# Making the up projection's weight sums by adding transfers in DRAM, and loading the latents' weights block by block

## The chip, the cores and the metric

The kernel runs on one core of a Trainium2 chip. Its engines work side by side, each through its own instructions in order: TensorE (PE, matrix products into PSUM), VectorE (DVE), ScalarE (ACT), GpSimd (POOL) and SyncE (SP, which issues most transfers). Transfers run on 16 DMA engines. Those issued by GpSimd go through the software queue, those issued by SyncE through the hardware queue. The metric is the device time of one execution in microseconds, the median of several.

## The reference

One layer of an encoder over 2048 + 256 tokens of width 1024, in float32, in two parts, each with a norm before and after it and a residual:

```python
h = rms_norm(x, g_mix_pre)
z = h @ w_in                       # latents (416 columns), then nq, nk, nv (512 columns each)
a = mla_attention(c_q, c_kv, k_rope, ...)    # long attention: 8 heads, every token with every token
n = neighborhood_attention(nq, nk, nv, na_rpb)   # 8 heads, windows on a 64-wide grid
mix = jnp.concatenate([a, n], axis=-1) @ w_o
x = x + rms_norm(mix, g_mix_post)
h = rms_norm(x, g_ffn_pre)
x = x + rms_norm(conv_ffn(h, w_ffn_up, ffn_conv_w, ffn_conv_b, w_ffn_down), g_ffn_post)

def conv_ffn(x, w_up, conv_w, conv_b, w_down):
    h = x @ w_up                                  # 1024 -> 2 * 2816
    hc = conv_b + (h at t-1, t, t+1) * conv_w     # width-3 convolution over the tokens
    g, u = jnp.split(hc, 2, axis=-1)
    return (jax.nn.gelu(g, approximate=True) * u) @ w_down
```

## The kernel before

Every product is made in three matmuls (`mm3`): each float32 factor is split into a high half (a cast on ScalarE, L95) and a low half (the difference, on VectorE, L96), and high x high, high x low and low x high are summed in PSUM. A scheduler lays down the order in which each engine works; it may take an instruction earlier than the code writes it, once its sources and its buffer are free.

The stages, in microseconds of the trace. The front, 0 to 240: nine blocks of 256 tokens. `norm_tile` loads 128 tokens, takes their squares (ScalarE), the factor (`rs_m` on VectorE, `rs_r` on GpSimd, L110), scales them (`xn`, L252), transposes them on TensorE into `pt` and splits them into `xh` and `xl`. A block then makes the values of all heads (`pv`) and the queries and keys of four heads (`pq`, stored through `qk_hl`). The weights for it come through four raw buffers (`load_w`, L182): W0 (512 columns, 8 loads), W1 and W2 (256 columns, 16 loads), and the second half of queries and keys for later (w3 here, 16 loads). The split x is kept in DRAM (`xs_d`).

The neighbourhood attention, 260 to 697: eight heads of nine grid units in two halves, 18 steps a head. GpSimd fetches the next head's tensors and the kept blocks of x. Beside the attention, TensorE first makes the other four heads' queries and keys (`queries_rest`), and from the middle (step 72) the latents of the long attention (`latents`). Their 416 columns of weights are loaded at step 72 through the `qk_hl` buffers into the place of the queries' weights, and the latents start six steps later.

Preparation and long attention, 697 to 1655, with almost no transfers. Output projection, 1659 to 1908: 18 tiles of 128 tokens; a tile's attention rows `at` are loaded from `att_d`.

The up projection, 1908 to 2940, works in 66 units (three groups of tokens by 22 columns of blocks j). A unit multiplies a 2 x 2 block matrix of weights with one of x by seven products in place of eight: a product m takes a factor of the weights (a raw block or a sum of blocks) and a factor of x, and VectorE and GpSimd put the results together. `ORDER` and `PLAN` give the order of the products, `pz` are their PSUM banks. The weights' factors are needed three times, once in each pass over j, so the sums are kept in DRAM (`ws_d`). `weight_sums` makes them for j = 0 to 5 on GpSimd beside the output projection (L138 loads, L149 sums, L144 stores); for j = 6 to 21 `w_source` makes them on GpSimd in the first pass (L1132) and stores them; the later passes load them (`load_w`, then split in `w_factor`). The down projection follows to 3505.

## Time and profile before

| | |
|---|---|
| median of 3 runs | 3513.39 us (3508.15 to 3514.28) |
| profiled execution | 3507.15 us, of it the span 3505.4 us |
| mean granted clock of TensorE | 0.989 of full speed |
| TensorE busy | 3368.9 us, 96% of the span |
| VectorE, ScalarE, GpSimd busy | 68%, 52%, 39% |
| transfers | 497.24 MB, mean 142 GB/s |
| of it through GpSimd's software queue | 76.10 MB in 35232 packets |

The page cuts the span into 40 slices; a digit is the busy share in tenths. TensorE is at 9 or 8 in almost all of them, so the other engines' times matter only where TensorE waits for them. The DMA digits show the stages: high in the front and the neighbourhood attention, near nothing in the long attention, high again in the output projection, about half in both projections of the second part.

### The profile page before, as it was taken

The page shows a single profiled execution, that of the slowest core. Times are in us where ns is not written, and L with a number is a line of the kernel's source. Part 1 is how long each engine was busy: PE and PEld are TensorE (multiplying, and loading weights), DVE is VectorE, ACT ScalarE, POOL GpSimd, SP SyncE. Part 2 cuts the span into 40 slices and gives each one's busy share as a digit, 9 for nine tenths or more (in the row PEclk, how much of TensorE's full clock was granted, in tenths as well). Part 3 has the DMA queues.
Part 4 walks back from the last instruction along what each step waited for, and adds up shares of the span by engine and source line. Part 5 has one row for each costly group of instructions (what it writes and reads, how often), then busy time and mean ns, then how long its engine had stood idle before and what let it go on. Part 6 is the DMA issues. An engine that isn't in the chain of part 4 may idle for free.

```text
span 3505.4 us, 51290 instructions
## 1 busy us (share of the span) xinstructions
PE 3368.9 (96%) x17806; PEld 2913.6 (83%) x17806; DVE 2385.9 (68%) x3774; ACT 1837.8 (52%) x3463; POOL 1376.2 (39%) x1216
## 2 busy tenths in 40 slices
PE   8999989989999999999989999899999999999999
PEld 7889979967777777766778999899989999888887
DVE  5325555588988888898345999987789776224332
ACT  4225556567777777777234544555555554223121
POOL 0022323157777778775521477632232222000110
PEclk9999999999999999999999999999999999999999
DMA  8789889341000000011995655465546555434553
GB/s 269 253 258 231 213 191 237 122 149 26 13 15 14 16 14 13 18 47 48 267 256 150 195 170 172 144 192 149 149 113 194 151 150 179 149 117 134 187 186 125
DMA packets 338068, 497.24 MB, mean 142 GB/s; under 512 B 69584, under 2 KB 213072, under 8 KB 330832
## 3 DMA queue, kind: packets, MB, share of 16 engines
q1 hardware_dynamic: 302576, 417.87, 39.7%
q0 software_dynamic: 35232, 76.10, 8.6%
q8 instruction: 140, 2.29, 0.3%
q14 instruction: 120, 0.98, 0.1%
HBM read 337.90 MB, written 155.37 MB: 141 GB/s over the span
## 4 chain that ended last, share of the span: by engine, by line
PE 74%; DVE 10%; ACT 6%; DMA 5%; issue 3%; POOL 2%; SPq 1%; ACTq 0%; POOLq 0%; DVEq 0%
PE pz L1291 21%; PE po L122 6%; PE po L120 6%; PE po L121 6%; PE po L646 3%; PE pS L619 3%; PE pg L600 3%; PE pl L647 3%; PE pS L621 3%; PE pS L620 3%; PE pO L448 2%; DVE wl L96 2%; PE pT L120 2%; PE pT L411 2%; PE pT L122 1%
## 5 line engine op out<-in xcount | busy, mean ns | idle before, releaser
L1291 PE MATMUL pz<-xh,wh 128*128 128x386 f32 (+1 forms) x1848 | 633.3, 343 | 20.8 <-DVE hg L1194 11.5
L1291 PE MATMUL pz<-xl,wh 128*128 128x386 f32 (+1 forms) x1848 | 630.2, 341 | 6.1 <-DVE xl L96 5.7
L1291 PE MATMUL pz<-xh,wl 128*128 128x386 f32 (+1 forms) x1848 | 628.8, 341 | 6.0 <-DVE wl L96 6.0
L634 POOL TENSOR_TENSOR acc<-acc,ph 128x512 f32<-128x512 f32 x434 | 568.3, 1309 | 103.8 <-ACT ph L623 82.3
L96 DVE TENSOR_TENSOR wl<-raw,wh 128x512 fp32r<-128x512 f32 (+1 forms) x470 | 444.0, 953 | 36.2 <-ACT wh L95 36.0
L95 ACT CAST wh<-raw 128x512 fp32r<-128x512 f32 (+1 forms) x470 | 288.9, 627 | 235.4 <-PE pz L1291 221.3
L623 ACT ACTIVATE ph<-pS 128x512 fp32r<-128x512 f32 (+1 forms) x528 | 312.4, 592 | 183.5 <-PE pS L621 98.6
L626 DVE TENSOR_TENSOR pl<-pS,ph 128x512 fp32r<-128x512 f32 (+1 forms) x528 | 354.6, 673 | 71.9 <-ACT pS L624 68.3
L110 POOL TENSOR_TENSOR rs_r<-rs_m,mhalf 128x1 f32<-128x1 f32 (+1 forms) x90 | 74.3, 826 | 800.4 <-DVE rs_m L107 800.1
L1291 PEld LDWEIGHTS pz<-xh,wh 128*128 128x128 f32 x1848 | 350.5, 190 | 31.3 <-DVE hg L1194 16.6
L1291 PEld LDWEIGHTS pz<-xl,wh 128*128 128x128 f32 x1848 | 351.1, 190 | 8.1 <-DVE xl L96 7.3
L1291 PEld LDWEIGHTS pz<-xh,wl 128*128 128x128 f32 x1848 | 350.7, 190 | 7.5 <-DVE wl L96 7.4
L602 DVE TENSOR_REDUCE mx<-pg 128x1 f32<-128x512 f32 (+1 forms) x528 | 343.0, 671 | 12.6 <-PE pg L600 10.1
L1241 POOL TENSOR_TENSOR cg<-cg,cu 128x768 f32<-128x768 f32 (+1 forms) x66 | 165.2, 2503 | 445.3 <-DVE cu L1225 324.6
L122 PE MATMUL po<-dh,xr 128*128 128x512 f32 x792 | 311.7, 394 | 0.4 <-DVE xr L96 0.4
L121 PE MATMUL po<-dl,xr 128*128 128x512 f32 x792 | 311.8, 394 | 0.0
L120 PE MATMUL po<-dh,xr 128*128 128x512 f32 x792 | 311.6, 393 | 0.0
L624 ACT ACTIVATE pS<-pS 128x512 f32<-128x512 f32 (+1 forms) x528 | 311.5, 590 | 0.0
L96 DVE TENSOR_TENSOR xr<-xt,xr 128x1408 fp32r<-128x1408 f32 x37 | 60.6, 1639 | 330.8 <-ACT xr L95 330.8
L95 ACT CAST xr<-xt 128x1408 fp32r<-128x1408 f32 x37 | 50.7, 1369 | 382.1 <-PE po L121 368.3
L619 PE MATMUL pS<-ql,kbh 96*128 96x512 f32 (+1 forms) x528 | 215.2, 408 | 5.0 <-DVE pl L626 2.9
L621 PE MATMUL pS<-qh,kbh 97*128 97x512 f32 (+1 forms) x528 | 211.8, 401 | 0.1
(259 smaller groups left out, 7923.6 us busy)
## 6 DMA issues: line engine op xcount, KB each, us to landing
raw<-ws_d SPq DMA_DIRECT2D x250, 256.0 KB, 2.7
raw<-in_w_ffn_up_dram SPq DMA_DIRECT2D x164, 256.0 KB, 3.2
xt<-g_d SPq DMA_DIRECT2D x37, 704.0 KB, 4.4
graw<-g_d SPq DMA_DIRECT2D x35, 704.0 KB, 5.1
g_d<-cg SPq DMA_DIRECT2D x110, 192.0 KB, 2.3
ws_d<-raw SPq DMA_DIRECT2D x80, 256.0 KB, 2.0
xl<-xs_d POOLq DMA_DIRECT2D x18, 1024.0 KB, 8.8
xh<-xs_d POOLq DMA_DIRECT2D x18, 1024.0 KB, 7.1
```

Of the source, the lines that this page charges most:

```text
L95: self.nc.scalar.copy(out=hi, in_=src)
L96: self.nc.vector.tensor_tensor(out=lo, in0=src, in1=hi.bitcast(F32), op=ALU.subtract)
L120: mm(out=out, lhsT=lh, rhs=rh, start=start, stop=False)
L121: mm(out=out, lhsT=lh, rhs=rl, start=False, stop=False)
L122: mm(out=out, lhsT=ll, rhs=rh, start=False, stop=stop)
L602: nc.vector.tensor_reduce(out=u.mx[:, i, c:c + 1], in_=pg[:, :n], axis=AX.X, op=ALU.max)
L619: mm(out=pS[:, :nq], lhsT=u.kh[0:QKD, kc], rhs=u.ql[:, :nq], start=True, stop=False)
L621: mm(out=pS[:, :nq], lhsT=u.kh[:, kc], rhs=u.qh[:, :nq], start=False, stop=True)
L623: nc.scalar.activation(out=ph[:, :nq], in_=pS[:, :nq], func=AF.Exp, scale=scale)
L626: nc.vector.tensor_tensor(out=pl[:, :nq], in0=pS[:, :nq], in1=ph[:, :nq].bitcast(F32), op=ALU.subtract)
L634: eng.tensor_tensor(out=u.acc[:, :nq], in1=ph[:, :nq].bitcast(F32), op=ALU.add, in0=u.p0[:, :nq].bitcast(F32) if j == 1 else u.acc[:, :nq])
L1291: nc.tensor.matmul(out=pz[:, :w], lhsT=l[:, kk, :], rhs=r[:, kk, :w], start=onto is None and kk == 0 and e == 0, stop=kk == 3 and e == 2, ...
```

## The change

The sums of weights are made without an engine: a transfer in DRAM copies one block of all weights of 11 columns j into `ws_d`, a second one adds the other block to it. The products are chosen so that four plain sums are left, of which two are built on another sum. So there are eight copies and eight additions, each of 11 x 128 x 512 numbers (2.88 MB), all issued by GpSimd. The code issues them at steps 20, 160, 270 and 360 of the long attention, four at a time, eight steps apart. What GpSimd did for the sums in the output projection and the first pass goes, with its loads and stores; all 66 units now load their factors alike.

In a unit the order of products is 1, 5, 3, 7, 2, 6, 4; six take a PSUM bank of their own (five before), and of the additions VectorE makes four instead of five and GpSimd one more.

The second half of queries' and keys' weights lies in eight tiles of 128 columns instead of two of 512. The latents' weights are loaded block by block through two buffers of their own (`load_lat`), each into a tile that the queries have left, from twelve steps before the middle on, and the latents start at the middle.

```diff
-        self.ws_d = scratch("ws_d", (NFF, 5, P, 512))
+        self.ws_d = scratch("ws_d", (NFF, 4, P, 512))
...
-    def weight_sums(self, raw_buf, out_buf, todo):
+    def weight_sums(self):
...
-                for m, ((r0, c0), (r1, c1), sign) in enumerate(self.WSUM.values()):
-                    nc.gpsimd.tensor_tensor(out=out[:, m], in0=raw[r0][:, c0], in1=raw[r1][:, c1],
-                                            op=ALU.add if sign > 0 else ALU.subtract)
-                outs.append((j, c, out))
-
-        def step():
-            load()
-            sums()
-
-        def flush():
-            while raws or outs:
-                sums()
-
-        return step, flush
+        block = lambda rc, js: a["w_ffn_up"].rearrange("(r j) p k c -> r j p (k c)", r=2)[
+            rc[0], js, :, 512 * rc[1]:512 * rc[1] + 512]
+        first, stages = [], [[], [], []]
+        for i, (m, (b0, b1)) in enumerate(self.WSUM.items()):
+            for js in (slice(0, 11), slice(11, NFF)):
+                first.append(lambda i=i, b0=b0, js=js: nc.gpsimd.dma_start(out=self.ws_d[js, i], in_=block(b0, js)))
+                src = self.ws_d[js, list(self.WSUM).index(b1)] if isinstance(b1, int) else block(b1, js)
+                stages[max(0, i - 1)].append(
+                    lambda i=i, src=src, js=js: nc.gpsimd.dma_start(out=self.ws_d[js, i], in_=src, accum_op=ALU.add,
+                                                                  max_dma_last_dim=2048))
+        return [first] + stages
...
-            w2 = w_tiles(w2p, 3, 512)
+            w2 = [[w2p.tile([P, KD, P], F32R, name=f"w{2 * f + i}") for i in range(2)] for f in range(4)]
...
-                        load_w(raw_buf, w2, LAT + 512 * (b - 2) + 256, 256, 256 * (b - 2))
+                        load_w(raw_buf, lambda k: [[w[:, k, :] for w in w2[2 * (b - 2) + i]] for i in range(2)],
+                               LAT + 512 * (b - 2) + 256, 256)
...
+            def load_lat(k):
+                raw = lwp.tile([P, LAT], F32, name="raw")
+                nc.sync.dma_start(out=raw, in_=a["w_in"][k * P:(k + 1) * P, 0:LAT])
+
+                def convert():
+                    wlat[k] = w2p.tile([P, 2, LAT], F32R, name=f"w{k}")
+                    self.split(raw, wlat[k][:, 0, :], wlat[k][:, 1, :])
+
+                return convert
...
+                if 0 <= i - (mid - 10) < KD:
+                    lat_w[i - (mid - 10)]()
+                if 0 <= i - (mid - 12) < KD:
+                    lat_w[i - (mid - 12)] = load_lat(i - (mid - 12))
+                if i == mid - 4:
+                    Rest.blocks = {0: fetch(0)}
                 if i == mid:
-                    wlat = [w[:, :, :LAT] for w in w_tiles(w2p, 3, 512)]
-                    Rest.n, Rest.blocks = 0, {0: fetch(0)}
-                    load_w(lambda: st.tile([P, 2, NB], F32, name="qk_hl").rearrange("p a b -> p (a b)"), wlat, 0, LAT)
-                if i >= mid + LATE and Rest.n < 4 * NT:
+                    Rest.n = 0
+                if i >= mid and Rest.n < 4 * NT:
...
+            for q, part in enumerate(self.weight_sums()):
+                for r, f in enumerate(part):
+                    later.setdefault((20, 160, 270, 360)[q] + 8 * r, []).append(f)
...
-        sums, flush = self.weight_sums(lambda: buf(0, 6, 512), lambda: buf(1, 2, 1280),
-                                       [(j, c) for j in range(self.NSUM) for c in range(2)])
...
-            if t < 7:
-                sums()
-                sums()
-            if t == 7:
-                flush()
...
-    ORDER = (1, 5, 3, 4, 2, 7, 6)
-    WSUM = {1: ((0, 0), (1, 1), 1), 2: ((1, 0), (1, 1), 1), 5: ((0, 0), (0, 1), 1), 6: ((1, 0), (0, 0), -1),
-            7: ((0, 1), (1, 1), -1)}
-    WRAW = {3: (0, 0), 4: (1, 1)}
-    XSUM = {1: ((0, 0), (1, 1), 1), 3: ((0, 1), (1, 1), -1), 4: ((1, 0), (0, 0), -1), 6: ((0, 0), (0, 1), 1),
+
+    WSUM = {4: ((0, 1), (1, 1)), 5: ((0, 0), (0, 1)), 1: ((0, 0), 4), 2: ((1, 0), 1)}
+    WRAW = {3: (0, 0), 6: (1, 0), 7: (1, 1)}
+    XSUM = {1: ((0, 0), (1, 1), 1), 3: ((0, 1), (1, 1), -1), 4: ((0, 0), (1, 0), -1), 6: ((0, 0), (0, 1), 1),
             7: ((1, 0), (1, 1), 1)}
     XRAW = {2: (0, 0), 5: (1, 1)}
 
     PARTS = [(0, 770, 384, 0), (768, 770, 384, 768), (1536, 772, 386, 1536)]
 
-    PLAN = [(k, m) for k in range(3 * NFF) for m in (1, 5, 3, 4, 2, 7, 6)]
-    PLAN[4:9] = [(1, 1), (1, 5), (0, 2), (0, 7), (0, 6)]
-    NRAW = 13
-
-    NSUM = 6
+    PLAN = [(k, m) for k in range(3 * NFF) for m in (1, 5, 3, 7, 2, 6, 4)]
+    PLAN[4:9] = [(1, 1), (1, 5), (0, 2), (0, 6), (0, 4)]
+    NRAW = 10
...
-        if self.NSUM <= k < NFF:
-            for rc in {1: [(0, 0), (1, 1)], 5: [(0, 1)], 3: [(1, 0)]}.get(m, []):
-                t = self.blocks[k, rc] = self.ff_raw.tile([P, 4, P], F32, name="raw")
-                nc.sync.dma_start(out=t, in_=a["w_ffn_up"][j + rc[0] * NFF][:, 4 * rc[1]:4 * rc[1] + 4, :])
-            return
...
-        self.nc.gpsimd.tensor_tensor(out=t, in0=self.blocks[k, b0], in1=self.blocks[k, b1],
-                                     op=ALU.add if sign > 0 else ALU.subtract)
-        self.nc.sync.dma_start(out=self.ws_d[k, list(self.WSUM).index(m)], in_=t.rearrange("p a b -> p (a b)"))
...
-        self.w_source(i + 2)
...
+        def value(u):
+            tt(nc.vector, u.hu[:, 1, :u.w], u.b[6][:, :u.w], u.t[:, :u.w], 1)
+            u.cu = conv(u.hu, NFF + u.j, u.n, "u")
+
         def gate(u):
-            tt(nc.vector, u.hg[:, 0, :u.w], u.b[1][:, :u.w], u.v[:, :u.w], 1)
+            tt(nc.vector, u.hg[:, 0, :u.w], u.v[:, :u.w], u.b[7][:, :u.w], -1)
             u.cg = conv(u.hg, u.j, u.n, "g")
             nc.scalar.activation(out=u.cg[:, :, :u.n], in_=u.cg[:, :, :u.n], func=AF.Gelu_apprx_tanh)
-
-        def value(u):
-            tt(nc.vector, u.hu[:, 1, :u.w], u.b[3][:, :u.w], u.t[:, :u.w], 1)
-            cu = conv(u.hu, NFF + u.j, u.n, "u")
-            nc.gpsimd.tensor_tensor(out=u.cg[:, :, :u.n], in0=u.cg[:, :, :u.n], in1=cu[:, :, :u.n], op=ALU.mult)
+            nc.gpsimd.tensor_tensor(out=u.cg[:, :, :u.n], in0=u.cg[:, :, :u.n], in1=u.cu[:, :, :u.n], op=ALU.mult)
...
-            onto = {7: 1, 6: 3}.get(m)
+            onto = {4: 7}.get(m)
...
-            if m in (5, 4) or (m == 1 and k != 1):
+            if m in (1, 5, 7):
                 keep(u, m)
             if m == 3:
                 u.hg = hp.tile([P, 2, 388], F32, name="hg")
                 tt(nc.vector, u.hg[:, 1, :w], u.b[3][:, :w], u.s[5][:, :w], 1)
-            if m == 4:
                 u.v = hp.tile([P, 388], F32, name="v")
-                tt(nc.gpsimd, u.v[:, :w], u.s[4][:, :w], u.s[5][:, :w], -1)
+                tt(nc.gpsimd, u.v[:, :w], u.s[1][:, :w], u.s[5][:, :w], -1)
             if m == 2:
+                u.t = hp.tile([P, 388], F32, name="t")
+                tt(nc.vector, u.t[:, :w], u.v[:, :w], u.b[2][:, :w], -1)
                 u.hu = hp.tile([P, 2, 388], F32, name="hu")
-                tt(nc.vector, u.hu[:, 0, :w], u.b[2][:, :w], u.s[4][:, :w], 1)
-                u.t = hp.tile([P, 388], F32, name="t")
-                tt(nc.vector, u.t[:, :w], u.s[1][:, :w], u.b[2][:, :w], -1)
-                if k == 0:
-                    keep(hidden[1], 1)
+                tt(nc.gpsimd, u.hu[:, 0, :w], u.s[7][:, :w], u.t[:, :w], -1)
```

How the change moves instructions shows at three places. VectorE at the start of the program, before: `rs_m` and `xn` are the norm of a tile, `w0l` to `w2l` low halves of the front's weights.

```order
L107 TENSOR_SCALAR rs_m<-ss 128x1
L252 SCALAR_TENSOR_TENSOR xn<-x,rs_r,g_mix_pre_b 128x1024
L96 TENSOR_TENSOR w0l<-raw,w0h 128x512 x4
L107 TENSOR_SCALAR rs_m<-ss 128x1
L252 SCALAR_TENSOR_TENSOR xn<-x,rs_r,g_mix_pre_b 128x1024
L96 TENSOR_TENSOR xl<-pt,xh 128x8x128
L107 TENSOR_SCALAR rs_m<-ss 128x1
L96 TENSOR_TENSOR w0l<-raw,w0h 128x512 x2
L252 SCALAR_TENSOR_TENSOR xn<-x,rs_r,g_mix_pre_b 128x1024
L96 TENSOR_TENSOR w0l<-raw,w0h 128x512 x2
L96 TENSOR_TENSOR xl<-pt,xh 128x8x128
L96 TENSOR_TENSOR w1l<-raw,w1h 128x256 x2
```

VectorE at the start, after (the rows left out are 28 more of the narrow low halves, `w_82<-raw,w_81` to `w_88<-raw,w_87`, which are the second half of queries' and keys' weights):

```order
L107 TENSOR_SCALAR rs_m<-ss 128x1
L96 TENSOR_TENSOR w0l<-raw,w0h 128x512 x4
L107 TENSOR_SCALAR rs_m<-ss 128x1
L96 TENSOR_TENSOR w0l<-raw,w0h 128x512 x4
L96 TENSOR_TENSOR w1l<-raw,w1h 128x256 x8
L96 TENSOR_TENSOR w2l<-raw,w2h 128x256 x8
L96 TENSOR_TENSOR w_82<-raw,w_81 128x128
L96 TENSOR_TENSOR w_84<-raw,w_83 128x128
L96 TENSOR_TENSOR w_82<-raw,w_81 128x128
...
L96 TENSOR_TENSOR w_88<-raw,w_87 128x128
L233 SCALAR_TENSOR_TENSOR xn<-x,rs_r,g_mix_pre_b 128x1024 x2
```

The norm of the first tile, second in the row before, now stands behind the low halves of all 40 raw loads, and the norms of tiles 0 and 1 stand together.

VectorE at the border of two blocks of the front, before: `v` are a block's values, `qk_hl` the low halves of its queries and keys, `xl` the low half of a normed tile.

```order
L96 TENSOR_TENSOR v<-pv,v 128x8x64 x2
L96 TENSOR_TENSOR xl<-pt,xh 128x8x128
L107 TENSOR_SCALAR rs_m<-ss 128x1
L252 SCALAR_TENSOR_TENSOR xn<-x,rs_r,g_mix_pre_b 128x1024
L197 SCALAR_TENSOR_TENSOR qk_hl<-pq,qk_hl 128x256 x2
L96 TENSOR_TENSOR xl<-pt,xh 128x8x128
L107 TENSOR_SCALAR rs_m<-ss 128x1
L252 SCALAR_TENSOR_TENSOR xn<-x,rs_r,g_mix_pre_b 128x1024
L96 TENSOR_TENSOR qk_hl<-pq,qk_hl 128x256 x2
```

The same place, after:

```order
L96 TENSOR_TENSOR v<-pv,v 128x8x64 x2
L177 SCALAR_TENSOR_TENSOR qk_hl<-pq,qk_hl 128x256 x2
L96 TENSOR_TENSOR qk_hl<-pq,qk_hl 128x256 x2
L233 SCALAR_TENSOR_TENSOR xn<-x,rs_r,g_mix_pre_b 128x1024 x2
L96 TENSOR_TENSOR xl<-pt,xh 128x8x128
L107 TENSOR_SCALAR rs_m<-ss 128x1
L96 TENSOR_TENSOR xl<-pt,xh 128x8x128
```

Before, the norms of the next block (`xn`) stand between the two pairs of `qk_hl`; after, both stand behind the fourth `qk_hl` of the block, and TensorE's transposes of them with them. That is so at the borders after blocks 0, 1, 2, 3, 5 and 6; after blocks 4 and 7 a norm still stands ahead.

GpSimd in the front and at the start of the neighbourhood attention, after: `rs_r` is a norm's factor, `ws_d<-in_w_ffn_up_dram` at L134 a copy and at L137 an addition, `xh` and `xl<-xs_d` fetch a kept block of x, and `q`, `kk`, `kl`, `v` a head's tensors.

```order
L134 DMA ws_d<-in_w_ffn_up_dram 11x128x512
masks.py:199 ISA
masks.py:199 AFFINE_SELECT ident<-ident 128x128
L110 TENSOR_TENSOR rs_r<-rs_m,mhalf 128x1 x2
L134 DMA ws_d<-in_w_ffn_up_dram 11x128x512
L110 TENSOR_TENSOR rs_r<-rs_m,mhalf 128x1 x2
...
L443 DMA xh<-xs_d 128x2048
L443 DMA xl<-xs_d 128x2048
L137 DMA ws_d<-in_w_ffn_up_dram 11x128x512
L200 DMA q<-naq_d 128x512
L203 DMA kk<-nak_d 64x512 x2
L203 DMA kl<-nak_d 64x512 x2
```

Before, GpSimd has only the factors here, and then the fetches and head loads. After, the eight copies stand between pairs of factors, the first ahead of the identity matrix's last step, and the additions stand one by one among the fetches and head loads (the last of the eight in the preparation of the long attention); none is left in the long attention.

## Rows read from the trace of the kernel before

**Rows 1.** The page's chain that ended last, share of the span by engine
```profile
PE 74%; DVE 10%; ACT 6%; DMA 5%; issue 3%; POOL 2%; SPq 1%; ACTq 0%; POOLq 0%; DVEq 0%
```

**Rows 2.** Windows, front: us, busy time (instructions), granted clock, DMA share, GB/s
```profile
0.00:20.00 20.00, 7.81 (x25) 6.11 (x26) 10.68 (x19) 12.36 (x20) 2.75 (x9) 1.00 0.79 268
43.50:240.00 196.50, 193.53 (x1261) 176.17 (x1259) 67.27 (x114) 54.88 (x105) 18.33 (x31) 0.99 0.77 249
120.00:140.00 20.00, 18.14 (x114) 16.66 (x113) 6.13 (x10) 5.74 (x10) 3.23 (x6) 0.91 0.71 212
```

**Rows 3.** Timeline of the start: start, duration, engine, line, idle and releaser
```profile
7.73 2.56 ACT L95 CAST w0h<-raw 128x512 fp32r<-128x512 f32 x4
8.46 1.28 DVE L252 SCALAR_TENSOR_TENSOR xn<-x,rs_r,g_mix_pre_b 128x1024 f32<-128x1024 f32 x1 [0.68 <-POOL rs_r L110]
9.67 2.49 DVE L96 TENSOR_TENSOR w0l<-raw,w0h 128x512 fp32r<-128x512 f32 x4
11.96 0.99 ACT L95 CAST xh<-pt 128x1024 fp32r<-128x1024 f32 x1
13.00 0.80 PE L120 MATMUL pv<-w0h,xh 128*128 128x512 f32 x1 [1.23 <-ACT xh L95]
14.11 1.22 DVE L96 TENSOR_TENSOR xl<-pt,xh 128x1024 fp32r<-128x1024 f32 x1
20.69 0.75 DVE L96 TENSOR_TENSOR w1l<-raw,w1h 128x256 fp32r<-128x256 f32 x2
43.09 0.42 DVE L96 TENSOR_TENSOR qk_hl<-pq,qk_hl 128x256 fp32r<-128x256 f32 x1 [1.08 <-ACT qk_hl L95]
```

**Rows 4.** The raw loads' line: duration min/median/max in ns, first and last start
```profile
L182 SPq DMA_DIRECT2D raw<-in_w_in_dram x40: 327/430/1707, 1.7 to 98.5; - x40
```

**Rows 5.** Windows of the neighbourhood attention's middle, columns as in rows 2
```profile
480.00:520.00 40.00, 26.86 (x150) 24.74 (x151) 20.04 (x46) 21.09 (x51) 7.87 (x13) 0.79 0.92 181
520.00:540.00 20.00, 20.00 (x143) 19.27 (x142) 11.76 (x30) 12.12 (x30) 5.24 (x5) 1.00 0.38 127
```

**Rows 6.** Chain of 470 to 520 us: start, duration, what
```profile
478.16 10.13 DMA qk_hl<-in_w_in_dram
```

**Rows 7.** Windows of the output projection, columns as in rows 2
```profile
1660.00:1820.00 160.00, 142.96 (x676) 117.24 (x677) 68.56 (x95) 45.13 (x71) 70.36 (x93) 0.96 0.93 267
1820.00:1880.00 60.00, 60.00 (x306) 50.63 (x305) 29.11 (x42) 21.46 (x36) 8.32 (x15) 1.00 0.67 180
```

**Rows 8.** TensorE's waits, 1660 to 1820 us: total, times, longest
```profile
PE pt L948 <- DMA at<-att_d: 15.5, 4, 7.1
```

**Rows 9.** Windows of the up projection, columns as in rows 2
```profile
2000.00:2200.00 200.00, 189.32 (x1041) 183.00 (x1040) 200.00 (x199) 94.66 (x162) 150.84 (x87) 1.00 0.53 170
2400.00:2500.00 100.00, 100.00 (x567) 100.00 (x566) 74.22 (x108) 54.92 (x88) 22.78 (x14) 1.00 0.55 152
```

**Rows 10.** Lines, 2000 to 2100 us, then 2400 to 2500: busy, mean ns
```profile
L96 DVE TENSOR_TENSOR wl<-raw,wh 128x512 fp32r<-128x512 f32 x44 | 56.3, 1291 | 0.0
L1132 POOL TENSOR_TENSOR raw<-raw 128x512 f32<-128x512 f32 x31 | 51.8, 1671 | 28.4 <-DVE wl L96 27.5
...
L96 DVE TENSOR_TENSOR wl<-raw,wh 128x512 fp32r<-128x512 f32 x48 | 35.2, 734 | 7.5 <-ACT wh L95 7.5
```

**Rows 11.** The page's DMA issues: times, KB each, median us to landing
```profile
xl<-xs_d POOLq DMA_DIRECT2D x18, 1024.0 KB, 8.8
...
raw<-in_w_in_dram SPq DMA_DIRECT2D x32, 128.0 KB, 3.1
...
raw<-in_w_in_dram SPq DMA_DIRECT2D x8, 256.0 KB, 5.0
```

**Rows 12.** Windows of the neighbourhood attention, columns as in rows 2
```profile
260.00:280.00 20.00, 17.86 (x120) 17.13 (x121) 11.02 (x27) 10.67 (x26) 5.33 (x9) 0.83 1.34 296
280.00:480.00 200.00, 194.40 (x1554) 187.11 (x1553) 113.89 (x277) 112.38 (x273) 57.96 (x83) 1.00 0.83 217
```

**Rows 13.** The fetches of x: duration in ns, first and last start
```profile
L460 POOL DMA_DIRECT2D xl<-xs_d x18: 528/538/576, 216.4 to 660.9; - x18
```

More of the change, by code (lines that the diff above doesn't have):

```diff
@@ L284, in queries @@
                         pq = ps.tile([P, 512], F32, name="pq")[:, :NB]
-                        qk_products(W[1 + f // 2], f % 2, pq, range(KD), xh, xl)
+                        qk_products([w[:, :, f % 2 * P:f % 2 * P + P] for w in W[1 + f // 2]], pq, range(KD), xh, xl)
                         qk_store(f // 2, 2 * (f % 2), pq, b)
@@ L475, in queries_rest @@
                     Rest.pq = ps_t.tile([P, 512], F32, name="pT")[:, :NB]
-                qk_products(w2, f, Rest.pq, range(4 * half, 4 * half + 4), *Rest.blocks[b])
+                qk_products(w2[f], Rest.pq, range(4 * half, 4 * half + 4), *Rest.blocks[b])
                 if half == 1:
@@ L1070, in ffn_pools @@
             self.xc_open(self.up, m)
-        self.xsrc, self.xc, self.raws, self.blocks, self.wf = {}, {}, {}, {}, {}
+        self.xsrc, self.xc, self.raws, self.wf = {}, {}, {}, {}
     def xc_open(self, stack, m, **k):
@@ L1187, in ffn @@
         wp = [en(name="ff_w0", bufs=3), en(name="ff_w1", bufs=5)]
-        for m in (3, 4):
+        for m in (3, 7):
             self.xc_open(right, m, side="right")
@@ L1275, in ffn @@
                 pz_open(2)
-                for q in (2, 7, 6):
+                for q in (2, 6, 4):
                     self.xc_open(self.up, q)
@@ L1313, in ffn @@
                     store = None
-            if m == 7:
-                if k < last:
-                    gate(u)
-                else:
-                    post.append(lambda: gate(u))
             if m == 6:
@@ L1321, in ffn @@
                     value(u)
+                else:
+                    post.append(lambda: value(u))
+            if m == 4:
+                if k < last:
+                    gate(u)
                     store = lambda u=hidden.pop(k): store_of(u)
                 else:
-                    post += [lambda: value(u), lambda: store_of(u)]
+                    post += [lambda: gate(u), lambda: store_of(u)]
         self.up.close()
```

63 lines of the change are left out of this document (17 added, 46 removed).

## The prediction

> **What bounds the kernel now.** I read the chain of waits first: three quarters of it are TensorE's own work [rows 1], so anything that doesn't hold TensorE up is free, and what counts is where TensorE stops. I then looked at the span in windows, one stretch per stage, for the columns that fall below full busy or below full clock. Four places matter here.
>
> The start: TensorE is busy for 7.81 of the first 20 us and then full [rows 2]. The timeline shows why it is so early: the norm of the first tile runs on VectorE at 8.46 us and the low halves of the weights only follow, so that the first product starts at 13.00 and the last store of block 0 is made at 43.09 [rows 3]. The 40 raw loads of projection weights are issued between 1.7 and 98.5 us [rows 4].
>
> The middle of the neighbourhood attention: between 480 and 520 us TensorE does 150 matmuls in 40 us where the next stretch does 143 in 20 [rows 5]; the chain there is a DMA of 10.13 us that brings the latents' weights [rows 6].
>
> The output projection: 676 matmuls in 160 us against 306 in the 60 us after, with the DMA engines at 0.93 of their time [rows 7]; TensorE waits 15.5 us for a load of attention rows [rows 8].
>
> The up projection's first pass: VectorE is busy 200 of 200 us and TensorE does 1041 matmuls; later 567 per 100 us, with VectorE at 74 [rows 9]. A low half of a weight takes 1291 ns there beside GpSimd's sums, and 734 ns without them [rows 10].
>
> **What the change does, part by part.**
>
> *Gains.* (1) The 60 sums in the output projection and their loads and stores go. At the rate of the later stretch (306/60 = 5.1 per us) 676 matmuls take 132.5 us, so 27.5 us are lost [rows 7]. The ends are the 15.5 us of the wait alone [rows 8] and 27.5; I take 25, since the DMA load that the wait stands for goes almost wholly.
> (2) The 80 sums and 80 stores of the first pass go, and the VectorE additions per unit fall from five to four. A unit is 84 matmuls: 84/5.205 = 16.14 us in the first pass, 84/5.67 = 14.81 after it [rows 9]; sixteen units (j = 6 to 21) save 16 x 1.33 = 21 us. Ends 15 and 25 (the two passes' borders could move a few us). The new order of products and the sixth bank add nothing, as TensorE is already full in the later passes.
> (3) The latents' weights come block by block and early. 150 matmuls at 143 per 20 us are 21 us, so 19 of the 40 us are lost [rows 5]; I take 12, as the conversions still stand among the attention's own work, with 3 and 19 as ends.
> Together 58 us, between 33 and 71.
>
> *Cost at the start.* The order of the changed program has the adding transfers not in the long attention, where the code writes them, but as early as their sources allow: the eight copies in the front, the eight additions one by one in the neighbourhood attention. And with the copies among GpSimd's norm factors the whole front comes in another order. On VectorE all 56 splits of projection weights (8 wide, 16 half as wide and 32 narrow ones) now stand ahead of the first norm; SyncE issues all 40 raw loads in one go through four buffers. An engine takes its work in order, so the first norm waits for the last raw load. One buffer's turn is its load, the cast, the split and the issue: for the eight wide loads 5.0 + 0.64 + 0.62 + 0.43 = 6.69 us, of which four run at once, so 1.67 each; for the 32 small ones 3.1 + 0.37 + 0.37 + 0.43 = 4.27, so 1.07 each [rows 3, 4, 11] (of a small cast no row is shown; it is taken to be as long as its split). The first norm starts at 1.7 + 8 x 1.67 + 32 x 1.07 = 49 us, and with two copies beside the loads say 52, against 8.46. From there block 0 runs as before. Cost: 43 us; less 2 for the two tiles of block 1 that block 0 no longer transposes: 41. Lowest: the issues alone (1.7 + 40 x 0.43 = 19) and some 9 us of splits behind them, so 28, which costs 20. Highest: loads that take twice as long beside the copies, near 80, which costs 70.
>
> *Cost at the block borders.* Before, the next block's norms stand between the queries of this one. Now, at six of eight borders (all but 4 to 5 and 7 to 8), they stand behind its last store. TensorE then waits for the cast and the low half (0.42 each, the cast taken to be as long), the norm (1.28), the cast of the transposed tile (0.99) and most of its low half (0.75 of 1.22, as two matmuls go ahead of it): 3.9 us; the transposes between are work that was there before [rows 3]. A stop also costs clock: between 120 and 140 us TensorE stood for 20 - 18.14 = 1.9 us, and the granted clock of that stretch is 0.91, a part of it at 1.2 instead of 2.4 GHz: another 1.8 us [rows 2]. So 6 x 5.7 = 34 us; ends 23 (no clock lost) and 48 (the wait for GpSimd's factor beside it).
>
> *Cost of the transfers.* No row of before shows a copy within DRAM or an adding transfer. Each moves 2.88 MB. From below: at the 296 GB/s of 260 to 280 us, with the DMA engines over full [rows 12], 10 us; that stretch is the nearest row. In the front the engines are busy 0.77 of the time [rows 2], so the copies fit beside TensorE's work, at the price of later loads: I take 4 us (0 to 20). In the neighbourhood attention, 0.83 busy [rows 12], an addition stands in GpSimd's queue ahead of the next block of x or the next head. A block's fetch takes 8.8 us [rows 11], and the fetches come 26 us apart (444.5 us for 17 steps) [rows 13], so a delay of 10 us is mostly covered: 2 us for each of the seven there, with the last in the preparation of the long attention 15. Without that cover, 9 us each, 65; below zero nothing speaks for it, as these transfers release nothing earlier.
> The Trainium skill speaks against them: *Collectives: The Full Stack*, "The bandwidth ceiling: the fold count and why AG ≠ RS ≠ AR", says that an addition in a DMA costs no time itself but reads two sources, so it runs at about half of a copy's rate. No run here shows it; with it an addition would be an estimated 20 us, twice the 10 from the row, and the exposed sum would be nearer to the upper end.
>
> *Sum.* 41 + 34 + 4 + 15 = 94 lost, 58 gained: 36 us slower. The profiled execution took 3507.15 us and would take 3543; the median shown is 6.2 above it, so the forecast is 3549. The long attention, with hardly any DMA, and the down projection stay as they are.
>
> **Rivals.** *The queue is held (B).* Software transfers run one behind another. If an addition takes 20 us or more, or GpSimd can't go on while one is being queued, each of the seven holds a fetch past its block, or a norm's factor in the front. For it: the DMA engines are 0.83 taken there before anything is added [rows 12]. Against it: 26 us between two fetches [rows 13]. It adds 50 us, seven waits of 9 less the 13 already counted: 3600.
> *The front hides it (C), faster or even.* The mechanism is the turn of the four raw buffers: nothing else but two copies uses the DMA engines then, and if the loads land near the issue rate the norm starts at 28 us and the start costs 20. With 23 at the borders and nothing for the transfers, 43 stand against 58: 3513 - 15 = 3498; with the upper gains 3485. The sign turns once start, borders and transfers together cost less than 58 us: with 23 and 4 for the last two that is a first norm before 42 us. For it: four raws are there and being cast at 7.73 us, with the first x [rows 3]. Against it: the splits behind the loads, and the order itself.
>
> **How the numbers follow.** Forecast 0.50, with a range of its own of 3515 to 3590; B 0.25; C 0.25. A run of this kernel varies by about 0.2% (3508 to 3514), so within 7 us counts as the same. Slower takes all of B, 0.45 of the forecast's half and a little of C: 0.72; same 0.06; faster 0.22. The range runs from 3480 (C with good gains) to 3625 (B with 75 us).
>
> **What would show it.** Right at the start: VectorE's first norm near 50 us and TensorE idle until then. At the borders: TensorE waits for xn, six times, 3 to 6 us. In the neighbourhood attention: waits for blocks of x at most a few us each. In the output projection the wait for attention rows gone and the rate over 100 matmuls per 20 us; in the first pass a unit of 14.8 us and VectorE well under full. The prediction is wrong if the first norm is early, if the fetches wait 20 us (B), or if the up projection's first pass keeps its 16.1 us.

## The result and the profile after

The changed kernel takes 3670.89 us (3664.74 to 3671.72) against 3513.02 us: 1.0448 times the time before [1.043, 1.0466]. The sign was forecast, the size not: 158 us lost instead of 36, outside the range.

Where the time went is read by stage, from the first and last start of each stage's products or scores in the two profiles (spans 3505.4 and 3669.5 us):

| stage | before | after | difference | forecast |
|---|---|---|---|---|
| start to the first score of the neighbourhood attention | 250.6 | 365.6 | +115.0 | +79 |
| neighbourhood attention, first to last score | 437.7 | 481.8 | +44.1 | +3 with the next |
| from there to the first score of the long attention | 101.1 | 122.2 | +21.1 | |
| long attention's scores | 862.9 | 862.8 | -0.1 | 0 |
| from the last score to the up projection (output projection) | 258.1 | 257.4 | -0.7 | -25 |
| up projection | 1034.7 | 1017.6 | -17.1 | -21 |
| the rest | 560.3 | 562.1 | +1.8 | 0 |

The front first. Windows of after, columns as in [rows 2]:

```profile
0.00:20.00 20.00, 0.00 (x0) 0.00 (x0) 4.03 (x11) 7.19 (x11) 4.27 (x10) 1.00 0.84 298
20.00:56.00 36.00, 0.00 (x0) 0.00 (x0) 16.88 (x52) 15.49 (x50) 0.00 (x0) 1.00 0.67 214
88.00:366.00 278.00, 230.28 (x1338) 203.37 (x1339) 69.42 (x112) 52.48 (x94) 31.70 (x48) 0.86 0.78 247
340.00:360.00 20.00, 3.83 (x18) 3.83 (x19) 3.95 (x12) 0.75 (x2) 3.83 (x7) 0.63 0.78 194
```

TensorE stands for 56 us, where it was at work from 13 us on [rows 3]. Over the blocks behind the first the mean granted clock is 0.86, where [rows 2] had 0.99, and at the end TensorE all but stops for 20 us. VectorE's timeline names the first stop and the border after block 0:

```profile
55.57 2.48 DVE L233 SCALAR_TENSOR_TENSOR xn<-x,rs_r,g_mix_pre_b 128x1024 f32<-128x1024 f32 x2
...
87.95 0.43 DVE L96 TENSOR_TENSOR qk_hl<-pq,qk_hl 128x256 fp32r<-128x256 f32 x1 [0.23 <-ACT qk_hl L95]
88.29 2.47 DVE L233 SCALAR_TENSOR_TENSOR xn<-x,rs_r,g_mix_pre_b 128x1024 f32<-128x1024 f32 x2
```

The norm starts at 55.57 us (forecast: 52) and block 0 ends at 87.95 against 43.09 [rows 3]. The raw loads answer [rows 4]: all forty now go out by 52.6 us.

```profile
L161 SPq DMA_DIRECT2D raw<-in_w_in_dram x40: 327/328/626, 1.7 to 52.6; - x40
```

The neighbourhood attention, in windows: the whole of it and a stretch of it, then two stretches of the preparation of the long attention, the first all but 4 us ahead of the last addition (876.05 us), the second beside it.

```profile
365.00:847.00 482.00, 437.80 (x3077) 415.15 (x3076) 245.54 (x587) 251.96 (x604) 126.28 (x173) 0.94 1.00 225
600.00:640.00 40.00, 28.42 (x178) 25.55 (x177) 18.07 (x43) 16.89 (x43) 11.56 (x16) 0.90 1.04 228
860.00:880.00 20.00, 7.70 (x31) 6.39 (x32) 7.93 (x27) 9.59 (x35) 13.56 (x29) 0.56 0.33 95
880.00:900.00 20.00, 13.89 (x63) 10.31 (x62) 8.94 (x30) 8.59 (x28) 6.55 (x18) 0.86 0.87 187
```

The DMA share is 1.00 over the whole stage, where [rows 12] had 0.83 at full clock; in 600 to 640 us, after an addition, TensorE does 4.5 matmuls per us against 7.8 there. The transfers' own rows show what GpSimd spends on an issue (ns, min/median/max), the first and last start, and below the time from issue to landing, by line; L134 is the copies, L137 the additions:

```profile
L134 POOL DMA_DIRECT2D ws_d<-in_w_ffn_up_dram x8: 1116/1142/1324, 1.4 to 288.6; - x8
...
DMA to landing us min/median/max: 17.5/20.4/28.1
```

```profile
L137 POOL DMA_DIRECT2D ws_d<-in_w_ffn_up_dram x4: 1995/1998/2003, 312.3 to 594.8; - x4
L137 POOL DMA_DIRECT2D ws_d<-ws_d x4: 1942/1997/2015, 675.7 to 876.1; - x4
...
DMA to landing us min/median/max: 29.2/30.7/43.1
```

A copy needs a median of 20.4 us to land and an addition 30.7, where the forecast had 10. The waits of TensorE up to 1000 us (total, times, longest):

```profile
PE pt L237 <- DVE xn L233: 75.5, 8, 56.9
PE pt L841 <- DVE zn L824: 20.6, 4, 19.3
```

The first row is the start and seven later norms (18.6 us together). The second is the preparation, but 19.3 of its 20.6 us end at 872.30 us, before the last addition is issued; the seventh was issued at 800.41 and landed 30.1 us later. With copies alone (e3 below) TensorE stops for 8.5 us at this place: there VectorE makes the first `zn` behind one low half of the stage's weights, here behind all four, so that it waits for four loads in turn.

```profile
871.18 0.75 DVE L809 SCALAR_TENSOR_TENSOR wkl<-raw,gk,wkh 128x512 fp32r<-128x512 f32 x1 [3.42 <-ACT wkh L808]
871.85 0.35 DVE L824 TENSOR_SCALAR zn<-z,rs_r 128x256 f32<-128x256 f32 x1
```

Some 11 of the 25 us that the preparation loses against e3 thus go with the changed order. Behind the addition issued at 876.05 the chain of after then has two slow loads (start, duration, what); all loads of that table of rotations need 2.2 us at the median.

```profile
886.25 6.27 DMA z<-z_d
...
895.13 11.35 DMA cs<-in_rope_dram
```

In the neighbourhood attention TensorE's waits are spread (the largest group is 17.0 us in six). The chain of after has two additions themselves there, from issue to landing, and behind them GpSimd's loads of a head's keys and values:

```profile
594.79 32.59 DMA ws_d<-in_w_ffn_up_dram
...
675.73 29.41 DMA ws_d<-ws_d
```

The same is seen at GpSimd, which stood ahead of a head's values until an addition had landed, and at ScalarE, which waited for a buffer whose store was late:

```profile
POOL v L205 <- DMA ws_d<-ws_d: 21.2, 1, 21.2
```

```profile
ACT qk_hl L95 <- DMA naq_d<-qk_hl: 17.6, 5, 5.3
ACT o L434 <- DMA natt_d<-o: 14.4, 5, 5.3
```

The output projection and the up projection, windows that answer [rows 7] and [rows 9]:

```profile
1840.00:1860.00 20.00, 7.81 (x26) 5.75 (x27) 3.29 (x11) 1.21 (x2) 1.58 (x4) 0.59 0.67 184
1860.00:2080.00 220.00, 216.47 (x1073) 181.33 (x1072) 100.59 (x148) 72.98 (x120) 34.29 (x51) 0.99 0.61 170
2180.00:2380.00 200.00, 200.00 (x1131) 200.00 (x1130) 155.90 (x202) 110.27 (x173) 61.24 (x41) 1.00 0.50 153
```

The output projection runs at 97.5 matmuls per 20 us once it is going (84.5 before, in its first 160 us); from the first tile's last transposes (`pu`) to the last tile's it took 240.4 us and takes 222. But it now starts with a stop (1840 to 1860) that gives it all back. The first pass of the up projection runs at 5.66 matmuls per us, as forecast, with VectorE at 78%.

### The profile page after: what moved, and what is told of

Its sections match the earlier page's. It is cut to its first block, busy times and chain, and to the rows that moved or that the text cites. A ratio compares the mean times of both kernels' runs of the same rounds, so it can differ in the third digit from the quotient of the medians.

```text
span 3669.5 us, 51097 instructions
## 1 busy us (share of the span) xinstructions
PE 3409.6 (93%) x17806; PEld 2946.7 (80%) x17806; DVE 2332.7 (64%) x3724; ACT 1857.3 (51%) x3479; POOL 1297.4 (35%) x1158
## 4 chain that ended last, share of the span: by engine, by line
PE 73%; DMA 10%; DVE 8%; ACT 4%; issue 3%; POOL 1%; SPq 0%; ACTq 0%; POOLq 0%; DVEq 0%
PE pz L1254 24%; PE po L120 7%; PE po L122 7%; PE po L121 7%; PE po L644 3%; PE pS L617 3%; PE pg L598 3%; PE pl L645 2%; PE pS L619 2%; DMA naq_d<-qk_hl 2%; PE pS L618 2%; PE pO L431 1%; DVE wl L96 1%; DMA raw<-in_w_in_dram 1%; DVE mx L600 1%
## 5 line engine op out<-in xcount | busy, mean ns | idle before, releaser
L1157 POOL TENSOR_TENSOR v<-s,s 128x386 f32<-128x386 f32 (+1 forms) x66 | 101.5, 1538 | 435.7 <-DVE cg L1188 308.0
```

## The experiments

What a kernel leaves out is told in its expectation. Ratios are to the kernel before, on the same chip.

**No transfers: e1_no_transfers.** Theory: the loss sits in the transfers and the order that they bring. Rival: the rest of the change costs too.

```diff
-            for q, part in enumerate(self.weight_sums()):
+            for q, part in enumerate([]):
...
-            nc.sync.dma_start(out=flat, in_=self.ws_d[j, list(self.WSUM).index(m)])
+            r, c = {4: (0, 1), 5: (0, 1), 1: (0, 0), 2: (1, 0)}[m]
+            nc.sync.dma_start(out=t, in_=a["w_ffn_up"][j + r * NFF][:, 4 * c:4 * c + 4, :])
```

> The changed kernel without any of the sixteen transfers; the up projection loads raw blocks in place of the sums (so the weight sums are left out). Theory 1 (the large copies and additions that GpSimd issues, by the order they force and by their traffic, cost the whole loss): the front and the neighbourhood attention go back to the times of before, and the gains are left: about 3455 us (3440 to 3480). Rival (the new weight tiles, the latents' loads and the new order of products cost it): slower than 3513, with the first scores of the neighbourhood attention after 300 us.

Measured: 3473.38 us, 0.9907 [0.9889, 0.9926]. First norm at 8.71 us, first score at 249.3, neighbourhood attention 423.0, preparation 97.3, up projection 1014.6: nearly 200 us lie between this kernel and the changed one, and all of it comes with the sixteen transfers and the order that they bring. The theory's 3440 to 3480 holds. But the output projection's stage still takes 256.6 us, so its missing gain isn't the transfers' doing.

**The latents alone: b1_latents_only**, the kernel before with the weights' tiles and `load_lat` of the change and nothing else.

> The kernel before with the part on the latents' weights alone: tiles of 128 columns, loads block by block, latents from the middle on. From the stages of the kernel without transfers: neighbourhood attention 423 instead of 438 us, preparation 97 instead of 101, the rest as before: about 18 us less than the kernel before, ratio 0.995. Rival (that gain came from the absence of the sums' traffic or from another order): within 5 us of the kernel before.

Measured: 3490.96 us, 0.9956 [0.9944, 0.9969]. The neighbourhood attention takes 423.3 us instead of 437.7 and the preparation 98.2 instead of 101.1. The front of the profiled execution is 6.7 us longer (first score at 257.3), so its span is only 11.3 us shorter; by the medians it is 18. The stretch of [rows 5] is filled:

```profile
480.00:520.00 40.00, 39.77 (x275) 38.36 (x276) 24.67 (x61) 24.95 (x60) 10.30 (x18) 1.00 0.99 234
```

**Copies without additions: e3_copies_only.**

```diff
-            for q, part in enumerate(self.weight_sums()):
+            for q, part in enumerate(self.weight_sums()[:1]):
```

> The changed kernel with the eight copies where they are, without the eight additions (so one block is missing from each sum). Theory 1 and its rival agree on the front: first scores at about 365 us. If the additions cost what the neighbourhood attention and the preparation lost (44 and 21 us) it takes about 3605 us; if those came from the disturbed front order or the latents it stays near 3670.

Measured: 3579.31 us, 1.0202 [1.0186, 1.0219]. First norm at 55.52 us, first score at 351.4, neighbourhood attention 427.5, preparation 97.3. So the eight additions, with the order that they bring, cost 92 us by the spans (3669.5 - 3577.6): 14 at the end of the front (365.6 - 351.4), 54 in the neighbourhood attention, 25 in the preparation. The expectation had missed the first of these. The eight copies and the order of the front cost 106 more than e1 has. Two of ScalarE's waits in the neighbourhood attention, for comparison with after:

```profile
ACT qk_hl L95 <- DMA naq_d<-qk_hl: 9.9, 2, 7.0
...
ACT o L434 <- DMA natt_d<-o: 1.8, 2, 1.1
```

**The front's order without a transfer: e11_order_only**, as e1, with the front written in the changed order and each norm held behind the last low half of the raw loads or of the block before.

```diff
+                    with tc.issue_after(self.gate):
                         nc.vector.scalar_tensor_tensor(out=xn, in0=x, scalar=r[:, 0:1], in1=g,
```

> The kernel without any transfer (sums left out), its front forced into the changed kernel's order: all 40 raw loads and their splits ahead of the first norm, and each block's norms behind the last store of the block before, at all eight borders. Order theory: first norm at 45 to 50 us, first scores of the neighbourhood attention at 249 + 40 + 8 x 5.7 = 335 us, about 3558 us in all. Traffic theory (the copies' bytes made the first norm and the borders late): first scores before 300 us, under 3525 us.

Measured: 3551.39 us, 1.0139 [1.0116, 1.0161]. First norm at 40.26 us, blocks of 29 to 32 us (24.3 to 26.6 before), first score at 329.0: the order alone costs 80 us. It has all eight borders bad, the changed kernel six; without the two further ones (6.7 and 3.9 us) that would be 69. The first norm shows the copies: without them the forty loads are through 15 us earlier.

**Copies without the order: e5b_small_copies_only.** The same bytes, cut into 88 copies of one column j each; so cut, the front keeps its early norm.

```diff
-            for js in (slice(0, 11), slice(11, NFF)):
+            for js in [slice(j, j + 1) for j in range(NFF)]:
```

> As the kernel with copies only, the same bytes, but each copy cut into eleven of one column j, which leaves the first norm ahead of the weights' splits on VectorE and the next block's norms between the queries. Order theory (the place of the norms costs the front, not the copies' traffic): first norm near 8.5 us, first scores of the neighbourhood attention near 260 us, about 3470 us in all. Traffic theory (the copies' bytes slow the front's loads and stores): first scores later than 320 us, over 3540 us.

Measured: 3522.74 us, 1.0045 [1.003, 1.0059]. First norm at 9.92 us, first score at 296.3: between the two theories, the copies alone, so cut, cost 47 us of the front. They don't do it by GpSimd's factors, for which VectorE waits 2.9 us in the first 140 us, but by the front's own transfers: the raw loads of these 140 us need 7.3 us to land at the median, in e1 3.4, ScalarE waits 52 us for them instead of 8, and they are 37% of the chain there. Its window from 43 us on:

```profile
43.00:296.00 253.00, 220.11 (x1396) 200.38 (x1395) 75.83 (x152) 62.53 (x137) 54.59 (x101) 0.93 0.85 292
```

**All transfers cut small: e5_small_hoisted** (the same cut, with the additions). Cut so, the additions move into the front too.

> The changed kernel with all copies and additions as early as the scheduler likes, but each cut into eleven of one column j: the bytes of the changed kernel, an order close to the one without transfers. Against the copies-only version of the same cut (3523 us) only the additions are new. Order theory (what an addition costs in the neighbourhood attention is the order around it): neighbourhood attention 425 us from its first score to its last, preparation 98, about 3525 us in all. Traffic theory (its bytes and its place in the software queue): the 482 and 122 us of the changed kernel, about 3600 us.

Measured: 3604.94 us, 1.0287 [1.0265, 1.0309]; first score at 380.4, then 422.9 for the neighbourhood attention. The order theory had the neighbourhood attention, the traffic theory the total: the additions cost 84 us where they stand, which is now the front (380.4 - 296.3), where e5b's DMA engines are busy 0.85 of the time, and nothing behind it.

**Additions in the neighbourhood attention, TensorE's order kept: e15_additions_in_attention.** The transfers with the 128 rows outermost, each addition held behind a head's tables.

```diff
+        turn = lambda t: t.rearrange("j p c -> p j c")
...
+                    if t in self.sum_at:
+                        with tc.issue_after(self.tables[self.sum_at[t]]):
+                            t()
```

> The changed kernel with all sixteen transfers unchanged in size and number but described with the 128 rows outermost, and the additions held one by one behind a head's tables in the neighbourhood attention, so that they stand at almost the places of the changed kernel while TensorE's order there is almost that of the kernel without transfers (16 lines of difference in the products of that stage; the changed kernel has 392). What is open is whether the 54 us that the additions add in the neighbourhood attention (481.8 against 427.5 with copies only) and the 25 us in the preparation are the transfers' own (they hold GpSimd's queue and the DMA engines, so fetches come late) or come from the other order of TensorE's work. If the transfers' own: natt 470 to 490 us, preparation 115 to 125, GpSimd's fetches behind each addition waiting 15 to 25 us. If the order's: natt 425 to 440, preparation 97 to 105. The front has the copies and part of the bad order: its first score 290 to 330. In total about 3590 to 3620 by the first theory and 3530 to 3560 by the second.

Measured: 3564.06 us, 1.0158 [1.0131, 1.0186]; neighbourhood attention 452.3 us, preparation 97.5. Neither theory had it: 25 us (452.3 against 427.5) are lost beside an order as good as that without transfers; the other 29 go with the changed order or with the shape, which this run changes together (what the shape does to a transfer stands in the last section). On the chain of this run stand three fetches of x behind additions, of 24 to 26 us each, where e3's fetches need 10.5 at most, and TensorE waits 10.7 us for such fetches. The preparation loses nothing once the last addition is issued at 703 us, ahead of it. The window of the stage:

```profile
312.00:764.00 452.00, 423.00 (x3073) 405.73 (x3073) 244.85 (x586) 252.76 (x604) 130.35 (x176) 0.97 1.05 249
```

**In the long attention, as the code writes it: e2_pinned.** Each transfer is held behind GpSimd's last sum of the long attention's weights.

```diff
+                    if t in sums:
+                        with tc.issue_after(self.pool_ins):
+                            t()
```

> The changed kernel with every transfer queued behind a GpSimd instruction of the long attention, at the steps where the code writes it. Theory 1: as without the transfers, about 3460 us (3440 to 3480), since the DMA engines are at 0.08 there; TensorE in the long attention stays at 862 us. Rival (an addition in DRAM is dear wherever it stands, by holding GpSimd or the memory): the long attention takes over 20 us longer than its 862.

Measured: 3558.51 us, 1.0149 [1.0134, 1.0164]. Front and neighbourhood attention are as in e1 (253.9, 422.6), but the long attention takes 946.9 us instead of 862.7. The theory's 3440 to 3480 is missed, and the rival's sign is there. TensorE's order changes around the transfers: up to 13 score products of `pg` in a row, where e1 has at most three.

**Cut small, in the long attention: e7_pinned_small**, e2 with the cut of e5b; TensorE's order is that of e1.

> All transfers in the long attention, as in the pinned kernel, but cut into single columns, so that TensorE's order there is the one without transfers. Order theory: the long attention takes 863 us again instead of 947, about 3475 us in all, as without transfers; if 176 issues on GpSimd are too many for its free fifth, up to 20 us more. Traffic theory (the copies and additions slow the loads of the long attention): it stays near 940 us, over 3545 us.

Measured: 3526.16 us, 1.0066 [1.0044, 1.0088]; long attention 913.3 us. Neither theory had it. The large cut and its order are 34 of the 84 us; the other 51 are lost beside e1's order, and GpSimd is full in the stretches with the 176 issues. That these issues and not the bytes cost the 51 is argued from that, and from e12 below, where the same bytes cost 20. Windows of e7, and of e1 in the same place:

```profile
830.00:930.00 100.00, 93.80 (x405) 66.53 (x406) 83.71 (x146) 72.22 (x141) 98.69 (x113) 0.98 0.50 162
1080.00:1130.00 50.00, 40.44 (x167) 27.44 (x166) 32.90 (x57) 29.00 (x56) 50.00 (x50) 0.89 0.92 141
```

```profile
830.00:930.00 100.00, 98.58 (x444) 70.82 (x442) 88.76 (x156) 75.56 (x147) 80.30 (x63) 1.00 0.06 15
```

**The stores of zeros later: e9_pinned_small_zc**, e7 with the three stores `x_d<-zc` behind the fourth tile of the output projection. They take SyncE 6.55 us at 1844.72 us of after, ahead of the first load of neighbourhood rows:

```profile
1844.72 6.55 SPq L931 DMA_DIRECT2D x_d<-zc x3
1851.31 0.67 SPq L938 DMA_DIRECT2D na<-natt_d  x1
```

> The pinned kernel with small transfers, and the three narrow stores of zeros in the output projection moved behind its fourth tile, out of the way of the first loads of the neighbourhood attention's rows. Theory (the output projection's gain was lost to a late first load behind these stores on SyncE): its time from the last score of the long attention to the first product of the up projection falls from 256 us by 5 to 12 us, about 3466 us in all. Rival (these loads are late by themselves): no change against the pinned kernel with small transfers.

Measured: 3521.9 us, 1.0049 [1.0033, 1.0065]; from the last score to the up projection 250.3 us instead of 255.1. Just under the theory's 5 to 12: a part of the missing 25, not the most.

**Eleven raw buffers: e13_none_eleven_raws**, e1 with one number changed.

```diff
-    NRAW = 10
+    NRAW = 11
```

> The kernel without transfers (sums left out), with eleven raw buffers in place of ten, which in the order brings the output projection's zero stores and first loads back to the start of the long attention. Theory (the number of raw buffers moved these loads behind the last score, and that ate the output projection's gain): from the last score of the long attention to the first product of the up projection 238 us instead of 256, about 3455 us in all. Rival: no change, 3473 us.

Measured: 3462.65 us, 0.9874 [0.9855, 0.9893]; the stage takes 237.4 us instead of 256.6. The stores of zeros are at 784 us again, as before the change (795), and the output projection starts without a stop.

**Put together: e12_pfirst_pinned**, which leaves nothing out: sixteen transfers with the 128 rows outermost, held in the long attention and spread over it (a copy every 20 steps, an addition every 25), and eleven raw buffers.

```diff
+                    later.setdefault(at, []).append(f)
+                    at += (20, 25, 25, 25)[q]
```

> All sixteen transfers in the long attention, as large as in the changed kernel but with the 128 rows as the outermost dimension in place of the eleven columns, spread evenly, and eleven raw buffers in place of ten. With this shape TensorE's order in the long attention is the one without transfers. Theory (a transfer cost order there, and in the small cut GpSimd's issue time, not bytes): the long attention takes 863 to 873 us, and with the raw buffers the output projection gets its early first loads back; 3455 to 3470 us in all, faster than the kernel before. Rival (bytes or queue cost it wherever they go): the long attention over 900 us, 3500 us or more.

Measured: 3480.76 us, 0.9926 [0.9913, 0.9938]: 28 us faster than before on the same chip (3509.06), and some 190 faster than the changed kernel. The long attention takes 884.4 us, 20 more than in e13 and 11 above the theory's upper end, as is the total; the rest is as there. TensorE's order there is not quite the one without transfers: counted over the products in the two traces, it differs from e13's in some 190 lines (e2's from e1's in some 800). How much of the 20 us is order, issue or traffic isn't separated. Its window beside e1's above, and the transfers in this quiet stage:

```profile
830.00:930.00 100.00, 95.73 (x427) 67.66 (x427) 85.69 (x150) 77.01 (x150) 77.86 (x62) 1.00 0.33 102
```

```profile
L135 POOL DMA_DIRECT2D ws_d<-in_w_ffn_up_dram x8: 1064/1067/1143, 794.3 to 1034.6; - x8
...
DMA to landing us min/median/max: 11.7/12.3/13.3
```

```profile
L138 POOL DMA_DIRECT2D ws_d<-in_w_ffn_up_dram x4: 1851/1876/1947, 1064.9 to 1192.7; - x4
L138 POOL DMA_DIRECT2D ws_d<-ws_d x4: 1855/1874/1893, 1233.0 to 1359.2; - x4
...
DMA to landing us min/median/max: 18.8/19.6/20.9
```

## Why the prediction was right and wrong

*Latents, 12 forecast: 17.* The 14.4 and 2.9 us of b1. Right, nearer the upper end.

*Up projection's first pass, 21 forecast: 17.* Right; the rate is that of the later passes. VectorE's low halves still take 887 ns beside GpSimd's work and not 734, which costs nothing, as VectorE no longer sets the pace.

The front's 115 us are, by the ends of the blocks, 45 at the start, 53 at the six borders (7.6 us on average at five, 15.5 at the one after block 3) and 18 at the last block, of which 14 come with the first addition (e3); at the other places it gains 1.

*Start, 41 forecast: 45.* Right in mechanism: VectorE's first norm waits for forty raw loads. That the size is right too is luck in part: the copies beside the loads were put at 3 us and are 15 by e11, and the loads alone were put at 49 us, where the first norm of e11 starts at 40.

*Borders, 34 forecast: 53.* Right in mechanism, too small in size: e11 has 6.6 us a border without a transfer, 39 for these six, against 5.7 and 34. The other 14, for which this term had nothing, come with the transfers, most of them at the border after block 3, where two copies are issued (197 and 214 us) and ScalarE waits 11.4 us for stores of `qk_hl`.

*Copies, 4 forecast.* Mis-sized; their cost lies within the stretches above. Beside the bad order they add 22 (351.4 - 329.0), or 33 if e11's two further borders are taken off, the 15 at the start and the 14 at the borders among them; beside the good order they cost 47. The step that failed is "the copies fit beside TensorE's work": 0.77 of the DMA time taken [rows 2] was read as 0.23 free. But 23 MB are moved in some 300 us in which the front's own loads and stores have to land in time; in e5b the raw loads take 7.3 us instead of 3.4.

*Additions, 15 forecast: 93* (14 + 54 + 25). The largest miss, and the step that failed is "a delay of 10 us is mostly covered". An addition takes 31 us to land, not 10, which is more than the 26 us between two fetches [rows 13], and that cover was worked out for the fetches of x alone. In the changed kernel those hardly stop TensorE (4.0 us); what is late is the rest of GpSimd's queue and of the DMA engines' work: a head's keys and values behind two additions on the chain (32.6 and 29.4 us), stores that hold the `qk_hl` buffers (17.6 us against 9.9 in e3), stores of `o` (14.4 against 1.8), the rotation tables in the preparation. A second step had no term at all: the additions also change the order of the stages in which they stand, and that is some 11 of the preparation's 25 us. The upper end of 65 was built on fetches too, and so too low. Rival B had the mechanism, an addition of over 20 us that holds GpSimd's queue, but priced it by the fetches as well. Of the 54 us in the neighbourhood attention e15 gives 25 to transfers as such; whether the other 29 are the order's (392 lines of difference in TensorE's products) or the shape's isn't separated.

What the prediction drew from the Trainium skill pointed the right way. The Trainium skill, *Collectives: The Full Stack*, "The bandwidth ceiling: the fold count and why AG ≠ RS ≠ AR", says of a ring's ReduceScatter that its addition reads two sources and so runs at about half of a copy's rate; in the quiet long attention of e2 the copies ran at about 290 GB/s and the additions at 143. The 296 GB/s taken from [rows 12] was thus right for a copy, and the estimate of 20 us nearer to the truth for an addition than the 10 taken.

*Output projection, 25 forecast: 1.* The wait for attention rows went and the stage runs 18 us shorter from tile to tile (222 against 240.4), but the start lost as much. The step that failed is that the change's other numbers were put at nothing without a reason: NRAW from 13 to 10 moves the stores of zeros and the first load of rows from 800 us to behind the long attention's last score. Eleven buffers give 19 us of this stage back (e13); the whole kernel gains 11 by the medians (3462.65 against 3473.38), as other stages of the profiled execution are a few us longer. That the number of buffers decides it is shown; by which memory the tiles then share wasn't tried.

Rival C was off from both sides: the first norm came at 55 us, not 28, and the transfers weren't free.

## What to carry to other kernels

A transfer isn't free because an engine doesn't do it: set its time to land (here, for 2.9 MB, medians of 12 to 20 us for a copy and 20 to 31 for an addition) against the slack of every other load and store of the stage, not of one. Read where the scheduler has put it, not where the code writes it, and hold it in the stage with idle DMA engines; that, with the other description of the transfers and an eleventh raw buffer, turned 4.5% slower into 0.7% faster. Holding alone (e2) left it 1.5% slower. And a changed buffer count is part of the change: follow what it lets start early.

## What was not expected

How a transfer is described, with the same bytes, changed its rate. Additions in the quiet long attention: in slices of 1 us from 1076 us of e2 (11 columns outermost), where three run one behind another, then one in slices of 0.5 us from 1233 us of e12 (128 rows outermost); DMA is the engines' mean busy share in tenths:

```profile
DMA  0008698888777777777777799898777777797777
GB/s 0 0 0 39 80 169 158 150 144 154 136 136 138 138 145 141 142 143 145 139 145 145 137 156 147 139 154 144 143 143 143 141 145 143 144 182 145 141 140 138
```

```profile
DMA  0000093999999999999999999999999999758100
GB/s 0 0 0 0 0 78 29 152 180 152 193 217 201 209 213 201 209 213 201 209 213 205 209 209 201 213 201 217 205 209 201 217 197 217 127 104 203 28 0 0
```

143 GB/s with the DMA engines at 0.7, against 207 at 0.9 and more: 1.45 times, which is 16 to 11. The Trainium skill, *DMA: Bandwidth & Descriptors*, "Why a DMA increments its semaphore by 16 and not by 1", says that a transfer is spread over the largest number of engines up to 16 that divides the slowest dimension of both its sides, so over 11 here; the trace agrees. The copies of e2 show a share of 0.6 to 0.7 at 290 GB/s. The changed kernel's additions are described as those of e2, which the prediction didn't look at; 30.7 us to land there against 23.2 in e15 goes the same way.

The description changed the scheduler's order too, which is no matter of the chip: with columns outermost the engines' work is laid down another way around the transfers, in the front (first norm at 55.57 us, with rows outermost in e15 at 31.70) and in the long attention (e2 and e12).

GpSimd itself pays for each issue: 1.1 us for a large copy, 2.0 for a large addition, in e7 0.52 and about 1.5 for one column. With 176 small ones GpSimd was full and the long attention lost 51 us, with sixteen large ones, spread, 20.
